# The second product of two MLPs with tokens on partitions, in 2x2 blocks with seven block products

## The chip, the cores and the metric

One core of a Trainium2 chip runs the whole program. The metric is the time of one execution in microseconds (us) on the device, as the median of several runs. The engines are TensorE (PE in the profile, its weight loads PEld), VectorE (DVE), ScalarE (ACT), GpSimd (POOL) and SyncE (SP, which here issues most of the loads). Each takes its own list of instructions; semaphores order them among each other.

## What is computed

512 tokens of 1024 features in float32 go through two layers, each a token mixer and a squared-ReLU MLP of width 4096, both with RMSNorm ahead and a residual behind. The first mixer is an attention with forget gates (FoX), the second a latent attention (MLA). Only the MLPs, their surroundings and the closing norm matter here:

```python
def sq_relu_mlp(h, w_up, w_down):
    return jnp.square(jax.nn.relu(h @ w_up)) @ w_down
for layer in range(DEPTH):
    ...
    x = x + sq_relu_mlp(rms_norm(x, norm_ffn_g[layer]), ffn_w_up[layer], ffn_w_down[layer])
    if layer == N_A_LAYERS - 1:
        k_nope, k_rope, v_shared = mla_shared_kv(x, kv_norm_g, mla_w_kv_a, mla_kv_a_norm_g, ...)
return rms_norm(x, final_norm_g)
```

## The kernel before

Activations lie with features on partitions: eight tiles of 128 features x 512 tokens. PE multiplies float32r, so every float32 operand is split into two float32r parts, hi (a cast on ACT) and lo (the difference, on DVE), and a product of two operands is three matmuls (`three`, L184): hi hi, hi lo, lo hi. With `flip` the operands change places, and the output has tokens on partitions.

The weights come in pieces of 128 x 1024 elements (512 KB) in the order of their use. `piece` (L174) hands out the next and starts the one behind it: a load on SP's queue into `raw` (two buffers), the cast to `whi` (L168) and the difference `wlo` (L169), with three buffers each. `linear` (L201) makes 24 matmuls of 512 tokens from a piece. Other operands are 2 KB tiles of a pool of 40 (`rt`, L104) or 14 (`rt2`); scratch tiles come from a pool of eight (`tt`, L107). PSUM's eight banks are shared under three tags for the whole program (L94).

The order within each engine's list is not that of the text: the framework places the instructions by the text's order, what is ready, and which buffers are free.

`ffn` (L580) goes through the width in four chunks of 1024. For each of a chunk's eight up pieces, `linear` fills a bank; DVE takes the larger of it and 0 times 1/rms of the token (L601), ACT squares twice (L603, L604), and DVE takes the difference (L605). Then come eight down pieces, each added to the residual by DVE (L617). The sum of squares for the next norm is built as each x is finished (`square_sum`, L212). `rstd_of` (L221) sums it over partitions with small matmuls (L226) and finds 1/rms by Newton steps on POOL or DVE; `along_tokens` (L246) spreads it over the partitions with matmuls (L251). The second MLP does its last chunk's down pieces twice, for 256 tokens each; `finish` (L629) closes the first half while the second is multiplied.

Between the MLPs, MLA makes its six inputs (L704 to L718), one after the other, from x scaled by two gains (`hk`, `hm`, L651); the norm of the keys' input needs the first two of them, and the first values (`v_gen`, L724) need that norm.

## Time and profile before

| | us |
|---|---|
| three runs, lowest to highest | 1173.04 to 1174.48 |
| their median | 1174.44 |
| span of the profiled execution, from its first to its last instruction | 1170.7 |
| first MLP, roughly | 262 to 612 |
| MLA's inputs and first values | 612 to 680 |
| second MLP, roughly | 809 to 1158 |

The profile gives the span of its execution and no other time for it; the median lies 3.7 us above that span. A row of the timeline starts with the start and the duration in us; in brackets stands how long the engine was idle before, and what released it. Matmuls overlap, so that the distance from start to start counts and not the duration of one. A row of a table by stretches has the stretch, its length, the busy us and instructions of PE, PEld, DVE, ACT and POOL, the granted clock of PE as a share, the DMA share and GB/s.

### The profile page before, as it was taken

To read this page: it belongs to the slowest core of one execution; us is meant where nothing else is said; L and a number is where in the kernel's file an instruction comes from. 1 tells how busy PE (TensorE), PEld (TensorE's weight loads), DVE (VectorE), ACT (ScalarE), POOL (GpSimd) and SP (SyncE) were. 2 spreads that over 40 slices of the span, in tenths; PEclk is the share of its full clock that TensorE was granted. 3 is DMA by queue.
4 is the path that set the end of the run, shared out by engine and by line. 5 is a ranking of instruction groups with operands and counts; after the bars stand their busy time and mean duration, and the time that the engine had idled before them with its cause. 6 is when DMAs were issued, how large, how long until landed. Compare 5 with 4: busy or idle time off the path is not lost.

```text
span 1170.7 us, 14430 instructions
## 1 busy us (share of the span) xinstructions
PE 1147.6 (98%) x5652; PEld 947.2 (81%) x5652; DVE 657.5 (56%) x1179; ACT 482.9 (41%) x839; POOL 28.9 (2%) x96
## 2 busy tenths in 40 slices
PE   8999999999999999999999999999999999999996
PEld 6777887788888888888887778788888888888895
DVE  6788887774434434334466688736433443433465
ACT  5555655553313223223344566534322322422441
POOL 1000000001000000000002100001000000000002
PEclk9999999999999999999999999999999999999998
DMA  5332222162232332323342211233322323223253
GB/s 183 128 108 73 73 90 76 34 198 90 91 107 90 93 106 90 104 94 93 124 144 80 59 39 50 73 108 114 102 90 93 105 90 104 95 91 107 90 175 113
DMA packets 35779, 116.13 MB, mean 99 GB/s; under 512 B 4080, under 2 KB 5744, under 8 KB 35712
## 3 DMA queue, kind: packets, MB, share of 16 engines
q1 hardware_dynamic: 34704, 113.62, 30.3%
q0 software_dynamic: 320, 1.05, 0.3%
q8 instruction: 44, 0.72, 0.3%
q10 hardware_dynamic: 688, 0.55, 0.1%
q14 instruction: 23, 0.19, 0.1%
HBM read 110.98 MB, written 4.23 MB: 98 GB/s over the span
## 4 chain that ended last, share of the span: by engine, by line
PE 94%; DVE 2%; POOL 1%; DMA 1%; ACT 1%; issue 1%; SPq 0%; DVEq 0%; ACTq 0%; POOLq 0%
PE acc L191 14%; PE acc L192 14%; PE acc L193 14%; PE sc L193 7%; PE sc L191 7%; PE sc L192 7%; PE tp L191 6%; PE tp L193 6%; PE tp L192 6%; PE tp L314 3%; PE sc L499 2%; PE sc L767 1%; PE acc L187 1%; PE acc L188 1%; PE acc L189 1%; PE tp L515 1%
## 5 line engine op out<-in xcount | busy, mean ns | idle before, releaser
L168 ACT CAST whi<-raw 128x1024 fp32r<-128x1024 f32 (+2 forms) x190 | 196.6, 1035 | 533.7 <-issue 234.6
L191 PE MATMUL acc<-r,whi 128*128 128x512 f32 (+1 forms) x780 | 303.2, 390 | 5.1 <-ACT whi L165 5.0
L193 PE MATMUL acc<-r,wlo 128*128 128x512 f32 (+1 forms) x780 | 298.1, 382 | 0.1
L192 PE MATMUL acc<-r,whi 128*128 128x512 f32 (+1 forms) x780 | 298.2, 383 | 0.0
L169 DVE TENSOR_TENSOR wlo<-raw,whi 128x1024 fp32r<-128x1024 f32 (+2 forms) x190 | 228.6, 1203 | 51.8 <-ACT whi L168 51.5
L191 PEld LDWEIGHTS acc<-r,whi 128*128 128x128 f32 x780 | 147.1, 189 | 35.4 <-ACT whi L165 5.0
L193 PEld LDWEIGHTS acc<-r,wlo 128*128 128x128 f32 x780 | 147.1, 189 | 29.2 <-DVE wlo L169 0.4
L192 PEld LDWEIGHTS acc<-r,whi 128*128 128x128 f32 x780 | 147.3, 189 | 28.0 <-DVE r L209 1.2
L191 PE MATMUL sc<-r,whi 128*128 128x512 f32 (+1 forms) x320 | 121.4, 379 | 0.0
L191 PE MATMUL tp<-r,whi 128*128 128x512 f32 (+1 forms) x320 | 121.3, 379 | 0.0
L193 PE MATMUL sc<-r,wlo 128*128 128x512 f32 (+1 forms) x320 | 121.1, 378 | 0.0
L193 PE MATMUL tp<-r,wlo 128*128 128x512 f32 (+1 forms) x320 | 121.1, 378 | 0.0
L192 PE MATMUL tp<-r,whi 128*128 128x512 f32 (+1 forms) x320 | 121.1, 378 | 0.0
L192 PE MATMUL sc<-r,whi 128*128 128x512 f32 (+1 forms) x320 | 121.1, 378 | 0.0
L192 PEld LDWEIGHTS tp<-r,whi 128*128 128x128 f32 x320 | 60.2, 188 | 11.3
L192 PEld LDWEIGHTS sc<-r,whi 128*128 128x128 f32 x320 | 60.2, 188 | 11.2
L191 PEld LDWEIGHTS tp<-r,whi 128*128 128x128 f32 x320 | 60.2, 188 | 11.2
L193 PEld LDWEIGHTS tp<-r,wlo 128*128 128x128 f32 x320 | 60.2, 188 | 11.2
L193 PEld LDWEIGHTS sc<-r,wlo 128*128 128x128 f32 x320 | 60.2, 188 | 11.2
L191 PEld LDWEIGHTS sc<-r,whi 128*128 128x128 f32 x320 | 60.2, 188 | 11.2
L301 ACT ACTIVATE t<-t,sm 128x512 f32<-128x512 f32 (+3 forms) x96 | 53.3, 558 | 32.6 <-DVE sm L297 32.2
L617 DVE TENSOR_TENSOR x<-x,acc 128x512 f32<-128x512 f32 (+1 forms) x32 | 19.9, 621 | 78.9 <-PE acc L193 78.9
(141 smaller groups left out, 1304.5 us busy)
## 6 DMA issues: line engine op xcount, KB each, us to landing
raw<-wts SPq DMA_DIRECT2D x186, 512.0 KB, 3.5
nb<-csc SPq DMA_DIRECT2D x8, 512.0 KB, 4.3
t<-xT SPq DMA_DIRECT2D x8, 256.0 KB, 6.1
x<-xT SPq DMA_DIRECT2D x8, 256.0 KB, 4.6
xkeep<-x SPq DMA_DIRECT2D x8, 256.0 KB, 2.0
x<-xkeep SPq DMA_DIRECT2D x8, 256.0 KB, 5.7
raw<-wts SPq DMA_DIRECT2D x4, 384.0 KB, 3.1
outT<-t POOLq DMA_DIRECT2D x4, 256.0 KB, 2.7
```

The lines of the kernel that those rows point to most:

```text
L168: nc.scalar.copy(hi[:, :w], raw[:, :w])
L169: nc.vector.tensor_tensor(lo[:, :w], raw[:, :w], f32(hi[:, :w]), op=ALU.subtract)
L187: mm(dst, xhi, whi, start=start, stop=False)
L188: mm(dst, xhi, wlo, start=False, stop=False)
L189: mm(dst, xlo, whi, start=False, stop=stop)
L191: mm(dst, whi, xhi, start=start, stop=False)
L192: mm(dst, whi, xlo, start=False, stop=False)
L193: mm(dst, wlo, xhi, start=False, stop=stop)
L301: nc.scalar.activation(out=Ls[e][:, :n], in_=Ls[e][:, :n], func=AF.Exp, scale=-1.0, bias=m[:, e : e + 1], accum_out=rs[:, e : e + 1])
L314: nc.tensor.transpose(tp[:, j * P : (j + 1) * P], L[:, j * P : (j + 1) * P], ident)
L499: mm(scs[e][:, :n], a[rows, q], b2[rows, :n], start=st, stop=sp)
L617: nc.vector.tensor_tensor(x[f][:, t], x[f][:, t], dn, op=ALU.add)
```

## The change

The first product of an MLP stays as it is. The second is computed as tokens x features: `three` with `flip`. Its inner dimension of 4096 is cut into eight parts of 512. For the first seven, the left operand (512 tokens x 512) and the right one (512 x 1024) are cut in 2x2 blocks, and seven block products are formed from the blocks and from sums and differences of them (`PRODUCTS`, in Winograd's form), in chunks of two, two, two and one parts; the up products of the next chunk are spread between the block products. The left blocks are squares from ACT (Relu, then Square); DVE makes the sums in place (`left`, `right`). Every operand is split behind that. Two of the products stay in four banks through all seven parts, two are gathered in SBUF (`q5`, `q7`), three are added to the output at each chunk's end. `combine` adds up the rest, and `plain` does the eighth part with the usual eight products of blocks.

1/rms now comes in as a factor per partition, squared, where a product is added to the output (`add_to`). The first MLP's output is turned back by 32 transposes (`turned_half`), with x kept in DRAM meanwhile (`xmid`); MLA's six inputs run in two passes over halves of the features, in the order `KORDER`. The second MLP's input is turned by 32 transposes, and the closing norm works on tokens by partitions, one block of 128 at a time. Residual tiles come from the pool of 40; PSUM is divided anew for each stage. The output has the shape (512, 1024), and the weights are laid out for it on the host. The diff, cut:

```diff
+HALF = 512
+CHUNKS = (2, 2, 2, 1)
+PRODUCTS = (("p1", "A11", "B11"), ("q5", "S1", "T1"), ("p6", "S2", "T2"), ("x3", "S4", "B22"), ("q7", "S3", "T3"), ("x2", "A12", "B21"), ("x4", "A22", "T4"))
+STRAIGHT = {"x2": (0, 0), "x3": (0, 1), "x4": (1, 0)}
+KORDER = (4, 5, 6, 7, 0, 1, 2, 3)
...
+    out += [("ffn0", 1024)] * 32
+    out += [("ka", 1024)] * 6
...
+    def stage(name, **tags):
+        if psum:
+            psum["stack"].close()
+        psum["stack"] = ExitStack()
+        psum["pool"] = psum["stack"].enter_context(
+            tc.tile_pool(name=f"ps_{name}", bufs=1, space=bass.MemoryType.PSUM, reuse_waits="tile")
+        )
+        psum["tags"] = tags
...
-    def rstd_of(acc, dim, mult=1.0, alone=False):
-        """acc: squares summed over blocks of features; -> mult/rms per token on a partition [128, 4]."""
+    def rstd_of(acc, dim, mult=1.0, tag="tp"):
         nb = acc.shape[-1] // P
-        ss = bank("tp", (P, nb))
+        ss = bank(tag, (P, nb))
         for tb in range(nb):
             mm(ss[:, tb : tb + 1], acc[:, tb * P : (tb + 1) * P], ones, start=True, stop=True)
+        return rsqrt_mean(ss, dim, mult)
+    def rsqrt_mean(ss, dim, mult=1.0, alone=False):
+        nb = ss.shape[-1]
...
-            xf = xpool.tile([P, S], F32, tag=f"x{f}", name=nm("x"))
+            xf = f32(rt())
...
+    def ffn(acc, layer, tokens, after):
+        gname = f"ffn{layer}"
+        base = DOWN + layer * DFF * D
+        with ExitStack() as fs:
+            rawp = fs.enter_context(tc.tile_pool(name="mlp_raw", bufs=8, reuse_waits="tile"))
+            sp = fs.enter_context(tc.tile_pool(name="mlp_s", bufs=4, reuse_waits="tile"))
+            h = [scaled(x[k], gname, k) for k in range(KD)]
+            state_ = {"r2": None}
+            s, raws, s1, zs = {}, {}, {}, {}
+            def up_item(n):
+                up = bank("go" if n < 4 * CHUNKS[0] and n % 2 else "up")
+                linear(up, piece(gname), h)
+                if state_["r2"] is None:
+                    rs = rstd_of(acc, D, tag="go")
+                    r2 = state_["r2"] = small.tile([P, NB], F32, tag="r2", name=nm("r2"))
+                    nc.vector.tensor_tensor(r2, rs, rs, op=ALU.mult)
+                hf, at = divmod(n, HALF // P)
+                if at == 0:
+                    s[hf] = sp.tile([P, HALF // P, S], F32, tag="s", name=nm("s"))
+                t = tt()
+                nc.scalar.activation(out=t, in_=up, func=AF.Relu)
+                nc.scalar.activation(out=s[hf][:, at, :], in_=t, func=AF.Square)
+            def raw(hf, a, b):
+                if (hf, a, b) not in raws:
+                    t = rawp.tile([P, 2, S], F32, tag="q", name=nm("q"))
+                    at = base + (hf * 4 + a * 2 + b) * P * 2 * S
+                    nc.sync.dma_start(t, wts[at : at + P * 2 * S].rearrange("(p j c) -> p j c", p=P, j=2))
+                    raws[hf, a, b] = t
+                return raws[hf, a, b]
+            def sub(out, a, b):
+                nc.vector.tensor_tensor(out, a, b, op=ALU.subtract)
+            def right(hf, kind):
+                b11, b12, b21, b22 = ((lambda a=a, b=b: raw(hf, a, b)) for a in range(2) for b in range(2))
+                if kind == "B11":
+                    return b11()
+                if kind == "T1":
+                    sub(b11(), b12(), b11())
+                    return b11()
+                if kind == "T2":
+                    sub(b11(), b22(), b11())
+                    return b11()
+                if kind == "B22":
+                    return b22()
+                if kind == "T3":
+                    sub(b12(), b22(), b12())
+                    return b12()
+                if kind == "B21":
+                    return b21()
+                if kind == "T4":
+                    sub(b11(), b21(), b11())
+                    return b11()
+            def left(hf, kind):
+                a11, a12, a21, a22 = (s[hf][:, k::2, t * 256 : (t + 1) * 256] for t in range(2) for k in range(2))
+                if kind == "S1":
+                    s1[hf] = sp.tile([P, 2, S // 2], F32, tag="s1", name=nm("s1"), bufs=2)
+                    nc.vector.tensor_tensor(s1[hf], a21, a22, op=ALU.add)
+                    return s1[hf]
+                if kind == "S2":
+                    sub(s1[hf], s1[hf], a11)
+                    return s1[hf]
+                if kind == "S4":
+                    sub(s1[hf], a12, s1[hf])
+                    return s1[hf]
+                if kind == "S3":
+                    sub(a21, a11, a21)
+                    return a21
+                return {"A11": a11, "A12": a12, "A22": a22}[kind]
+            held, filled = {}, set()
+            def add_to(tb, o, src):
+                dst, r = tokens[tb][o], state_["r2"][:, tb : tb + 1]
+                if layer == 0 and (tb, o) not in filled:
+                    nc.vector.tensor_scalar_mul(dst, src, r)
+                    filled.add((tb, o))
+                else:
+                    nc.vector.scalar_tensor_tensor(out=dst, in0=src, scalar=r, in1=dst, op0=ALU.mult, op1=ALU.add)
+            def down_item(chunk, i, hf):
+                to, lk, rk = PRODUCTS[i]
+                begin, end = hf == chunk[0], hf == chunk[-1]
+                kept = to[0] == "p"
+                if kept:
+                    begin, end = hf == 0, hf == starts[-1] - 1
+                    if begin:
+                        held[to] = [bank("keep"), bank("keep")]
+                elif begin:
+                    held[to, "bank"] = [bank("go"), bank("go")]
+                zs = held[to] if kept else held[to, "bank"]
+                rsrc = right(hf, rk)
+                whi, wlo = zip(*(split(rsrc[:, j, :]) for j in range(2)))
+                lsrc = left(hf, lk)
+                lhi, llo = (tt([P, 2, S // 2]).bitcast(F32R) for _ in range(2))
+                split(lsrc, lhi, llo)
+                for b in range(2):
+                    t = slice(b * P, (b + 1) * P)
+                    for j in range(2):
+                        three(zs[b], whi[j], wlo[j], lhi[:, j, t], llo[:, j, t], begin and j == 0, end and j == 1, flip=True)
+                if kept or not end:
+                    return
+                for b in range(2):
+                    if to in STRAIGHT:
+                        ta, o = STRAIGHT[to]
+                        add_to(2 * ta + b, o, zs[b])
+                    elif (to, b) not in held:
+                        held[to, b] = f32(rt())
+                        nc.scalar.copy(held[to, b], zs[b])
+                    else:
+                        nc.vector.tensor_tensor(held[to, b], held[to, b], zs[b], op=ALU.add)
+            def combine():
+                for b in range(2):
+                    u = tt()
+                    nc.scalar.copy(u, held["p1"][b])
+                    q5, q7 = held["q5", b], held["q7", b]
+                    u2 = tt()
+                    nc.vector.tensor_tensor(u2, u, held["p6"][b], op=ALU.add)
+                    add_to(b, 1, u2)
+                    add_to(b, 1, q5)
+                    nc.vector.tensor_tensor(u2, u2, q7, op=ALU.add)
+                    nc.vector.tensor_tensor(q5, q5, u2, op=ALU.add)
+                    add_to(2 + b, 1, q5)
+                    add_to(2 + b, 0, u2)
+                    add_to(b, 0, u)
+            def plain(hf):
+                ws, hs = {}, {}
+                for o in (1, 0):
+                    for k in range(2):
+                        t = raw(hf, k, o)
+                        ws[k, o] = [split(t[:, j, :]) for j in range(2)]
+                for ta in range(2):
+                    for k in range(2):
+                        lhi, llo = (rt((P, 2, S // 2)) for _ in range(2))
+                        hs[ta, k] = split(s[hf][:, k::2, ta * 256 : (ta + 1) * 256], lhi, llo)
+                order = [(tb, o) for o in (1, 0) for tb in range(NB)] if layer == 0 else [(tb, o) for tb in range(NB) for o in (1, 0)]
+                for tb, o in order:
+                    pp = bank("go")
+                    t = slice(tb % 2 * P, tb % 2 * P + P)
+                    for m in range(4):
+                        k, j = divmod(m, 2)
+                        lhi, llo = hs[tb // 2, k]
+                        three(pp, *ws[k, o][j], lhi[:, j, t], llo[:, j, t], m == 0, m == 3, flip=True)
+                    add_to(tb, o, pp)
+                    after(tb, o)
+            starts = np.concatenate([[0], np.cumsum(CHUNKS)]).tolist()
+            ends = starts[1:] + [starts[-1] + 1]
+            ups = [[hf * 4 + j for hf in range(a, b) for j in range(4)] for a, b in zip(starts, ends)]
+            for n in ups[0]:
+                up_item(n)
+            for c in range(len(CHUNKS)):
+                chunk = list(range(starts[c], starts[c + 1]))
+                items = [(i, hf) for i in range(7) for hf in chunk]
+                todo = list(ups[c + 1])
+                room = max(len(items) - 3, 1)
+                for m, (i, hf) in enumerate(items):
+                    while todo and (len(ups[c + 1]) - len(todo)) * room <= m * len(ups[c + 1]):
+                        up_item(todo.pop(0))
+                    down_item(chunk, i, hf)
+                assert not todo
+            combine()
+            plain(starts[-1])
+    stage("mlp0", up=1, go=3, keep=4)
+    xmid = keep.tile([P, KD, S], F32, name="xmid")
+    for k in range(KD):
+        nc.sync.dma_start(xmid[:, k, :], x[k])
+    xkeep = keep.tile([P, KD, S], F32, name="xkeep")
+    ytok = [[f32(rt()) for _ in range(2)] for _ in range(NB)]
+    xnew, hk, hm = {}, {}, {}
+    closing = {}
+    def turned_half(o):
+        if not closing:
+            closing["acc"] = tt()
+        for f in range(4 * o, 4 * o + 4):
+            xf = xnew[f] = f32(rt())
+            nc.sync.dma_start(xf, xmid[:, f, :])
+            pp = bank("go")
+            for tb in range(NB):
+                nc.tensor.transpose(pp[:, tb * P : (tb + 1) * P], ytok[tb][o][:, (f % 4) * P : (f % 4 + 1) * P], ident)
+            nc.vector.tensor_tensor(xf, xf, pp, op=ALU.add)
+            hk[f] = scaled(xf, "kv", f)
+            square_sum(closing["acc"], xf, f == KORDER[0])
+        for f in range(4 * o, 4 * o + 4):
+            hm[f] = scaled(xnew[f], "mix1", f)
+            nc.sync.dma_start(xkeep[:, f, :], xnew[f])
+    ffn(acc, 0, ytok, lambda tb, o: turned_half(o) if tb == NB - 1 else None)
+    acc = closing["acc"]
+    stage("mla", acc=3, sc=2, tp=3)
+    rpstack = ExitStack()
+    rp2 = rpstack.enter_context(tc.tile_pool(name="rp2", bufs=RP2, reuse_waits="tile"))
...
+        six = [bank(t) for t in ("acc", "sc", "sc", "acc", "tp", "tp")]
+        srcs = [hk, hk, hk, hm, hm, hm]
+        kv_t, q_t = [], []
+        for part in range(2):
+            for n in range(3):
+                w = blocks(piece("ka"))
+                for m in range(2):
+                    q = 2 * n + m
+                    for j in range(4):
+                        k = KORDER[4 * part + j]
+                        three(six[q], *w[4 * m + j], *srcs[q][k], part == 0 and j == 0, part == 1 and j == 3)
+                    if part == 0:
+                        continue
+                    if q == 0:
+                        rs = rstd_of(acc, D)
+                    elif q == 1:
+                        rstd = rstd_tile(rs)
+                        kv_t = [evac(t) for t in six[:2]]
+                        kv_acc = squares(kv_t)
+                    elif q == 2:
+                        krh, krl = roped(evac(six[2]))
+                    elif q == 3:
+                        rs = rstd_of(kv_acc, KVR)
+                        q_t.append(evac(six[3]))
+                    elif q == 4:
+                        ckv = normed(kv_t, rstd_tile(rs), "kva")
+                        q_t.append(evac(six[4]))
+                    else:
+                        q_t.append(evac(six[5]))
...
+    stage("mlp1", up=1, go=3, keep=4)
+    xtok = [[f32(rt()) for _ in range(2)] for _ in range(NB)]
+    fpool = ctx.enter_context(tc.tile_pool(name="fin", bufs=1, reuse_waits="tile"))
+    gfin = fpool.tile([P, D], F32, name="gfin")
+    nc.scalar.dma_start(gfin, fing.partition_broadcast(P))
+    sums = fpool.tile([P, 2, NB], F32, name="sums")
+    def finish(tb, o):
+        junk = tt()
+        nc.scalar.activation(out=junk, in_=xtok[tb][o], func=AF.Square, accum_out=sums[:, o, tb : tb + 1])
+        if o:
+            return
+        ss = small.tile([P, 1], F32, tag="ss", name=nm("ss"))
+        nc.vector.tensor_tensor(ss, sums[:, 0, tb : tb + 1], sums[:, 1, tb : tb + 1], op=ALU.add)
+        rs = rsqrt_mean(ss, D, alone=True)
+        for oh in (1, 0):
+            t = tt()
+            nc.vector.scalar_tensor_tensor(out=t, in0=xtok[tb][oh], scalar=rs, in1=gfin[:, oh * S : (oh + 1) * S], op0=ALU.mult, op1=ALU.mult)
+            q = (nc.sync, nc.scalar)[oh]
+            q.dma_start(out[tb * P : (tb + 1) * P, oh * S : (oh + 1) * S], t)
+    for tb in range(NB):
+        for o in range(2):
+            pp = bank("go")
+            for j in range(4):
+                nc.tensor.transpose(pp[:, j * P : (j + 1) * P], x[4 * o + j][:, tb * P : (tb + 1) * P], ident)
+            nc.scalar.copy(xtok[tb][o], pp)
+    ffn(acc, 1, xtok, finish)
+    psum["stack"].close()
+    assert state["next"] == len(PIECES)
```

More of the change, by code (lines that the diff above doesn't have):

```diff
@@ L113, in trunk @@
     mm = nc.tensor.matmul
+    stage("fox", acc=3, sc=2, tp=3)
     gsb = const.tile([P, NG], F32, name="gsb")
@@ L567, in out_proj @@
         return acc
-    rp2 = ctx.enter_context(tc.tile_pool(name="rp2", bufs=RP2))
+    x = []
+    acc = out_proj("fo", [parts[k] for k in range(KD)], xT, outs)
+    def ffn(acc, layer, tokens, after):
[155 more added lines that the diff above has]
+            plain(starts[-1])
@@ L645, in trunk @@
-    acc = ffn(acc, "ffn0", "ffn0")
-    xkeep = keep.tile([P, KD, S], F32, name="xkeep")
-    for k in range(KD):
-        nc.sync.dma_start(xkeep[:, k, :], x[k])
-    hk = [scaled(x[k], "kv", k) for k in range(KD)]
-    hm = [scaled(x[k], "mix1", k) for k in range(KD)]
-    xstack.close()
     ctxs = []
@@ L677, in roped @@
             return split(a)
-        banks = iter(["acc", "sc", "sc", "tp", "tp", "acc"])
-        def down(name, hs):
-            pp = bank(next(banks))
-            linear(pp, piece(name), hs)
-            return pp
         def evac(src):
```

144 lines of the change are left out of this document (27 added, 117 removed).

## The prediction

> **What bounds the kernel now.** I read the page first (busy shares, then the chain that ended last), then the busy time by stretches, then PE's waits.
>
> ```profile
> span 1170.7 us, 14430 instructions
> PE 1147.6 (98%) x5652; PEld 947.2 (81%) x5652; DVE 657.5 (56%) x1179; ACT 482.9 (41%) x839; POOL 28.9 (2%) x96
> ...
> PE 94%; DVE 2%; POOL 1%; DMA 1%; ACT 1%; issue 1%; SPq 0%; DVEq 0%; ACTq 0%; POOLq 0%
> ```
>
> ```profile
> 0.00:235.00 235.00, 227.82 (x1265) 181.84 (x1266) 185.54 (x466) 136.38 (x303) 4.77 (x20) 1.00 0.30 95
> 262.00:612.00 350.00, 350.00 (x1553) 290.05 (x1552) 151.99 (x179) 110.77 (x145) 3.28 (x12) 1.00 0.33 102
> ```
>
> After the span the second table's columns are PE, PEld, DVE, ACT, POOL and the granted clock: in the first MLP (262 to 612) PE never rests, while DVE works 152 of 350 us. In the FoX stage DVE is at 185.54/235 = 79% and PE still loses only 7 us, most of it at the start. So each product that goes is worth its full pace, as long as DVE and ACT feed PE. What that pace is:
>
> ```profile
> 563.28 0.39 PE L191 MATMUL tp<-r,whi 128*128 128x512 f32 x1
> ...
> 568.72 0.39 PE L191 MATMUL acc<-r,whi 128*128 128x512 f32 x1
> ```
>
> ```profile
> 651.30 0.39 PE L187 MATMUL acc<-whi,r 128*128 128x512 f32 x1
> ...
> 651.98 0.39 PE L187 MATMUL acc<-whi,r 128*128 128x512 f32 x1
> ```
>
> ```profile
> 1110.09 0.28 PE L191 MATMUL acc<-r,whi 128*128 128x256 f32 x1
> ...
> 1112.48 0.28 PE L193 MATMUL acc<-r,wlo 128*128 128x256 f32 x1
> ```
>
> From the first to the second row lie 24 products: 5.44/24 = 0.2267 us each (the 0.39 overlap). With the operands exchanged (L187, the form that the change uses) three take 0.68, the same. With 256 columns twenty take 2.39, 0.1195 each, where half of 0.2267 is 0.1134.
>
> **The change, part by part.** *Products.* Each MLP has 32 pieces up and 32 down, 24 products each: 1536. Afterwards: 768 up; down, seven of eight 512-row parts with seven block products of 12 each (84 instead of 96), one part plain: 588 + 96 = 684. That is 84 fewer for each MLP, 168 x 0.2267 = **-38.1 us**. The last chunk in halves goes: 384 products x (0.1195 - 0.1134) = **-2.3**.
>
> ```profile
> 274.20 0.89 PE tp L251 x8
> ...
> 762.92 0.87 PE tp L314 x8
> ...
> 1145.83 0.71 PE tp L251 x4
> ...
> 1159.47 0.62 PE tp L226 x4
> ```
>
> These rows of the chain price the turning. The output now has tokens on partitions, so 32 transposes come at the end of the first MLP and 32 at the start of the second: 64 x 0.87/8 = **+7.0**. The row 1/rms along tokens is no longer built in the MLPs (two times 0.89), nor the first half's closing norm (about 0.62 + 0.71): **-3.1**.
>
> *The end.*
>
> ```profile
> 1157.77 0.28 PE L193 MATMUL acc<-r,wlo 128*128 128x256 f32 x1
> ...
> 1160.19 0.16 DVE L228 TENSOR_SCALAR rs<-tp 128x2 f32<-128x2 f32 x1 [0.77 <-PE tp L226]
> ...
> 1162.43 0.16 DVE L237 SCALAR_TENSOR_TENSOR rs<-rs,rs 128x2 f32<-128x2 f32 x1
> ...
> 1163.90 3.22 DVE L638 SCALAR_TENSOR_TENSOR t<-x,gsb,tp 128x256 f32<-128x256 f32 x8 [1.32 <-PE tp L251]
> ```
>
> From the last product's end (1158.05) to 1170.7 are 12.65 us. Afterwards: handover 0.3, add 0.7, square with its sum 0.9, sum of two 0.2, the same twelve small operations 2.4, two scalings of 512 columns 1.4, and the store as now (1167.12 to 1170.7, 3.6): 9.5, so **-3.1**.
>
> *VectorE, the price of the scheme.*
>
> ```profile
> 628.32 0.69 DVE L688 TENSOR_TENSOR t<-acc,rstd 128x512 f32<-128x512 f32 x1 [1.93 <-ACT rstd L257]
> 628.93 0.68 DVE L688 TENSOR_TENSOR t<-sc,rstd 128x512 f32<-128x512 f32 x1
> ```
>
> ```profile
> 563.48 0.69 DVE L601 SCALAR_TENSOR_TENSOR t<-tp,rstd 128x512 f32<-128x512 f32 x1 [2.71 <-PE tp L193]
> 564.38 1.22 DVE L169 TENSOR_TENSOR wlo<-raw,whi 128x1024 fp32r<-128x1024 f32 x1 [0.21 <-ACT whi L168]
> 565.53 0.68 DVE L605 TENSOR_TENSOR r<-t,r 128x512 fp32r<-128x512 f32 x1
> ```
>
> Start to start, DVE takes 0.61 for 512 columns and 1.15 for 1024. A block product needs three splits of 512 (1.8), T1 to T4 add 1.15, S1 to S4 0.6: 1.8 to 3.6 us, against 12 x 0.2267 = 2.72 of PE. The 5.44 us of each up product lie between them, with 1.15 of DVE. By chunks (PE / DVE): the first two 81.6 / 54, the third, with four up products instead of eight, 59.9 / 50, the last 40.8 / 30. The first two are below the FoX stage's 79%, so I cost them at nothing; the third is at 83%, for which I take 1.5 us in each MLP (from 0 to 5): **+3**.
>
> The weak place is behind the last chunk. After its last up product four block products are left, 10.9 us of PE. In that time DVE has in its order: the rest of x4's splits 1.8, eight evacuations 4.9, the sixteen operations of `combine` 9.8, then the eight weight splits of `plain` 4.9 and a first left split 0.6: 22. Perhaps 3 of that is done while `combine` waits for q7. PE then stands 22 - 10.9 - 3 = 8 us in each MLP: **+16** (bounds 0, if the splits of `plain` go first, and 22).
>
> A PE that stands loses clock too:
>
> ```profile
> 1160.00:1162.00 2.00, 0.08 (x1) 0.00 (x0) 1.46 (x9) 0.00 (x0) 0.00 (x0) 0.78 0.00 0
> 1162.00:1164.00 2.00, 1.22 (x4) 0.93 (x4) 0.58 (x4) 0.00 (x0) 0.00 (x0) 0.50 0.00 0
> ```
>
> The granted clock was 1.00 until PE ran dry at 1158, 0.78 on average two to four us later, then 0.50. How long it stays low under new work no row shows. I take as long as it took to fall, 3 us at half pace, 1.5 lost, for the two holes and the one below: **+4.5** (bounds 0 and 22, all of one `plain` at half pace). The Trainium skill, "TensorE: Matmul & The Clock Gate", Part 1, says that an idle window of about 3.4 us halves the clock, and that as long a busy one restores it; the fall agrees with the two rows. By its figure each hole would lose an estimated 1.7 us instead of 1.5, and the sum would be 0.6 us higher.
>
> *Start of MLA.* Its six inputs now run in two passes over halves of k (72 products each), so the first MLP's last features can arrive late; but 1/rms and the keys' norm come later.
>
> ```profile
> 617.68 0.95 PE L226 MATMUL tp<-ones,t 128*128 128x1 f32 x8
> ...
> 626.50 1.16 PE L251 MATMUL tp<-ident,rs 128*128 128x128 f32 x8 [2.27 <-POOL rs L243]
> ```
>
> ```profile
> 638.40 0.95 PE L226 MATMUL tp<-ones,t 128*128 128x1 f32 x8
> ...
> 644.84 1.16 PE L251 MATMUL tp<-ident,rs 128*128 128x128 f32 x8
> ```
>
> ```profile
> PE sc L191 <- ACT r L139: 1.0, 1, 1.0
> ```
>
> ```profile
> 660.92 1.16 PE L251 MATMUL tp<-ident,rs 128*128 128x128 f32 x8 [1.38 <-POOL rs L243]
> ```
>
> The norm chain (L226 to L251) takes 8.8 or 6.4 us. Now the first values (L187, 651.30) start 39.1 us after the MLP's last product (612.24). Afterwards: transposes 1.7, first pass 16.3, one output 2.7, chain about 7.5, to the keys' squares 4.5, second chain with its sum 7.4, norm and split about 4.3: 44.4, so +5.3. The queries' later waits (1.4 and 1.0) then have time: -2.4. Without the transposes already counted: **+1.2**. The operand pool holds 40 tiles; at each MLP's start the eight token tiles come before h in it: +1 each, **+2** (bounds 0 and 5).
>
> *Sum:* -38.1 - 2.3 + 7.0 - 3.1 - 3.1 + 3 + 16 + 4.5 + 1.2 + 2 = **-12.9**. The span of 1170.7 becomes 1157.8. The runs' median of 1174.44 lies 3.7 above the span; I keep that: **1161.5 us**.
> ```profile
> x<-xT SPq DMA_DIRECT2D x8, 256.0 KB, 4.6
> xkeep<-x SPq DMA_DIRECT2D x8, 256.0 KB, 2.0
> ```
>
> Transfers cost nothing: the weights are fetched once, at the 102 GB/s of the row above, on SP's queue as now. The eight stores and eight loads of `xmid` that come on it are of the size of these two; the stores lie beside the first up products, and the last four loads, which wait for operand tiles, land some 5 us after the plain part, beside the first pass of 16.3 us. Without that cover they would cost those 5.
>
> **Rivals.** *A, everything is covered.* The orders of DVE and ACT are made so that the splits of `plain` go ahead of `combine`: neither hole, clock nor third chunk, only -38.1 - 2.3 + 7.0 - 3.1 - 3.1 + 1.2 = -38.4: 1136. For it: 79% of DVE in FoX and a full PE. Against it: 22 us of work against 10.9.
>
> *B, slower: ACT's order.* Every up product is followed by a Relu and a Square on ACT, and the splits of the next block product are written behind them. If they also run behind them, PE stands after each up product that a block product follows, 24 times in each MLP.
>
> ```profile
> 563.30 1.05 ACT L168 CAST whi<-raw 128x1024 fp32r<-128x1024 f32 x1 [3.34 <-issue]
> 564.26 0.63 ACT L603 ACTIVATE r<-t 128x512 fp32r<-128x512 f32 x1
> 564.78 0.61 ACT L604 ACTIVATE t<-t 128x512 f32<-128x512 f32 x1
> ```
>
> ACT's 512 columns start every 0.52 us; Relu, Square and three casts are 2.6, times 48: +125 in place of the holes, 1174.4 - 36.4 + 125 = 1263. It decides from 36.4/48 = 0.76 us a place. Against it: the cast at 563.30 starts as a piece ends (563.28) and the third of its buffers comes free, so it is that of three pieces on; the text has it behind that ended piece's squares, yet it runs before them. The order is not the text's, and casts run ahead as far as buffers reach: 12 operand tiles beside those held, three block products. For it: that lead is short, and a queue that is once placed wrongly stays so (2.27 us at 626.50 is such a place). The Trainium skill's same page says in Part 2 that ScalarE and VectorE take their queues strictly in order. No run here shows the opposite, and the price above is for just that.
>
> *C, DVE lags through chunks three and four,* about 0.5 us more for each of their 42 block products: +21, 1182. It needs DVE at 100% where I count 83%.
>
> **How the numbers follow.** Forecast 0.47 (1147 to 1172), A 0.25 (1135 to 1147), B and C with its neighbourhood 0.20 (above 1177), between them 0.08, of which 0.06 lie within the 0.2%. Range 1136 to 1184: from A, which leaves nothing to cover, to C; only B's full form lies outside. A measurement tells 0.2%, 2.3 us, from no change: faster 0.74, same 0.06, slower 0.20.
>
> **What would show it.** Products in the profile: 168 fewer of 512 columns' worth, at 0.227 a piece; a wait of PE for DVE ahead of the plain part, 8 us, in both MLPs, with the clock at 0.5 behind it; about 9.5 us from the last product to the end; first values of MLA some 5 us later than now after the MLP's last product. Wrong it is if PE waits after up products (B), if DVE is at 95% in the third chunk (C), or if PE goes from Strassen's last product straight on to the plain part (A).

## The result and the profile after

The changed kernel takes 1270.62 us (median of four, 1269.95 to 1272.38), the kernel before 1173.74 beside it (1171.68 to 1174.48): the ratio is 1.0836, with a 95% interval of 1.0821 to 1.0852. It is slower by 97 us, where 12.9 less were forecast. The profiled execution has a span of 1269.1 us.

From the page of the changed kernel: its span, the engines' busy shares, and the engines in the chain that ended last.

```profile
span 1269.1 us, 14402 instructions
PE 1142.4 (90%) x5324; PEld 913.7 (72%) x5324; DVE 828.7 (65%) x1482; ACT 596.4 (47%) x1103; POOL 18.9 (1%) x80
...
PE 64%; DVE 6%; ACT 6%; issue 1%; DMA 1%; POOL 1%; DVEq 0%; SPq 0%; POOLq 0%; ACTq 0%
```

PE has less to do than before and stands longer: 127 us without work, 23 before. In the chain its share fell from 94% to 64%, but the shares of that row add up to 79% only, so that the row can't say what took the rest. No engine is full: DVE is at 65%, ACT at 47%. So no other engine became the bound; there are many waits. PE's waits in the changed kernel (us in total, times, longest):

```profile
PE up L203 <- ACT t L616: 61.0, 46, 1.4
PE go L201 <- DVE r L153: 12.2, 2, 8.2
PE sc L203 <- DVE r L790: 9.6, 1, 9.6
PE go L200 <- DVE r L153: 8.0, 1, 8.0
...
PE go L199 <- DVE r L790: 3.4, 1, 3.4
PE go L199 <- ACT t L152: 3.4, 2, 1.9
```

The first row has the sign of rival B: 46 times a product into `up` waits for the Relu (L616) of the up piece before. In the timeline of PE the place looks like this:

```profile
320.24 0.39 PE L203 MATMUL up<-r,whi 128*128 128x512 f32 x1
...
324.78 0.39 PE L205 MATMUL up<-r,wlo 128*128 128x512 f32 x1
326.57 0.50 PE L203 MATMUL up<-r,whi 128*128 128x512 f32 x1 [1.41 <-ACT t L616]
326.91 0.39 PE L204 MATMUL up<-r,whi 128*128 128x512 f32 x1
327.14 0.40 PE L205 MATMUL up<-r,wlo 128*128 128x512 f32 x1
327.37 0.39 PE L199 MATMUL go<-r,t 128*128 128x512 f32 x1
```

At 320.24 two block products have ended, and the rest of an up piece runs, until its last product at 324.78. What comes next on PE is not the block product that the text has there, but the first three products (L203 to L205) of the *next up piece*, and only then the block product (L199, into `go`). Those three need the bank `up`, the only one of its kind, and Relu hasn't read it out yet. The place costs 1.79 - 0.23 = 1.56 us start to start, and 0.11 at the next product. The mean of the 46 waits is a little shorter (61.0/46 = 1.33 against 1.41), so about 1.6 us a place, some 73 us in all.

The timeline of all engines over the same time says why Relu is late:

```profile
324.98 1.04 ACT L180 CAST whi<-raw 128x1024 fp32r<-128x1024 f32 x1 [9.51 <-PE up L204]
325.93 0.59 ACT L616 ACTIVATE t<-up 128x512 f32<-128x512 f32 x1
326.05 1.23 DVE L181 TENSOR_TENSOR wlo<-raw,whi 128x1024 fp32r<-128x1024 f32 x1 [9.86 <-ACT whi L180]
326.42 0.61 ACT L152 CAST t<-s 128x512 fp32r<-128x512 f32 x1
```

ACT and DVE have both been idle for over 9 us, and then everything comes at once. ACT's first instruction is the cast of a later weight piece (L180). Its buffer comes free with the ended piece's last L204, one product before the piece itself ends; so it stands ahead of Relu, for 0.95 us. Behind Relu stands the left split (L152) of the block product that should have run meanwhile. Its operand, a sum of two blocks (L656), was made by DVE at 287.43, long before.

### The profile page after: what moved, and what is told of

The parts are those of the page before. It is cut to its first block, busy times and chain, and to the rows that moved or that the text cites. A ratio compares the mean times of both kernels' runs of the same rounds, so it can differ in the third digit from the quotient of the medians.

```text
span 1269.1 us, 14402 instructions
## 1 busy us (share of the span) xinstructions
PE 1142.4 (90%) x5324; PEld 913.7 (72%) x5324; DVE 828.7 (65%) x1482; ACT 596.4 (47%) x1103; POOL 18.9 (1%) x80
## 4 chain that ended last, share of the span: by engine, by line
PE 64%; DVE 6%; ACT 6%; issue 1%; DMA 1%; POOL 1%; DVEq 0%; SPq 0%; POOLq 0%; ACTq 0%
PE up L203 9%; PE up L204 8%; PE up L205 7%; PE go L201 5%; PE go L199 5%; PE go L200 5%; ACT whi L180 3%; PE acc L203 2%; PE keep L199 2%; PE acc L204 2%; DVE r L678 2%; PE keep L200 2%; ACT t L616 2%; PE keep L201 2%; PE acc L205 2%
## 5 line engine op out<-in xcount | busy, mean ns | idle before, releaser
L180 ACT CAST whi<-raw 128x1024 fp32r<-128x1024 f32 (+2 forms) x118 | 120.4, 1022 | 301.9 <-PE up L204 203.5
L203 PE MATMUL up<-r,whi 128*128 128x512 f32 x448 | 180.1, 402 | 61.6 <-ACT t L616 61.0
L152 ACT CAST r<-q 128x512 fp32r<-128x512 f32 x212 | 126.8, 622 | 115.7 <-PE go L200 57.0
L204 PE MATMUL up<-r,whi 128*128 128x512 f32 x448 | 175.8, 392 | 3.6 <-DVE r L221 3.6
L205 PE MATMUL up<-r,wlo 128*128 128x512 f32 x448 | 175.1, 391 | 0.0
L153 DVE TENSOR_TENSOR r<-q,r 128x512 fp32r<-128x512 f32 x212 | 141.1, 687 | 35.9 <-ACT r L152 13.7
L203 PEld LDWEIGHTS up<-r,whi 128*128 128x128 f32 x448 | 84.4, 188 | 96.8 <-ACT t L616 80.5
L203 PE MATMUL acc<-r,whi 128*128 128x512 f32 x300 | 123.0, 413 | 5.0 <-ACT whi L177 5.0
L204 PE MATMUL acc<-r,whi 128*128 128x512 f32 x300 | 118.4, 396 | 0.0
L205 PE MATMUL acc<-r,wlo 128*128 128x512 f32 x300 | 118.4, 395 | 0.0
L199 PE MATMUL go<-r,t 128*128 128x512 f32 x280 | 110.0, 394 | 3.4 <-ACT t L152 3.4
L200 PE MATMUL go<-r,t 128*128 128x512 f32 x280 | 110.3, 394 | 0.0
L201 PE MATMUL go<-r,t 128*128 128x512 f32 x280 | 109.6, 393 | 0.0
L204 PEld LDWEIGHTS up<-r,whi 128*128 128x128 f32 x448 | 84.6, 189 | 20.5 <-DVE r L221 4.9
L205 PEld LDWEIGHTS up<-r,wlo 128*128 128x128 f32 x448 | 84.6, 189 | 17.7
L203 PEld LDWEIGHTS acc<-r,whi 128*128 128x128 f32 x300 | 57.1, 191 | 18.3 <-ACT whi L177 5.0
L205 PEld LDWEIGHTS acc<-r,wlo 128*128 128x128 f32 x300 | 56.9, 190 | 12.5 <-issue 0.4
L204 PEld LDWEIGHTS acc<-r,whi 128*128 128x128 f32 x300 | 57.1, 190 | 11.5 <-DVE r L221 1.2
```

What stands on the lines that cost most here:

```text
L152: nc.scalar.copy(hi, src)
L153: nc.vector.tensor_tensor(lo, src, f32(hi), op=ALU.subtract)
L180: nc.scalar.copy(hi[:, :w], raw[:, :w])
L199: mm(dst, xhi, whi, start=start, stop=False)
L200: mm(dst, xhi, wlo, start=False, stop=False)
L201: mm(dst, xlo, whi, start=False, stop=stop)
```

## The experiments

The runs, told in the order of the argument, fall into three groups: what makes the 46 waits, what makes the holes between the stages, and what the form is worth alone. "Before" was between 1171.7 and 1173.4 us beside them.

### E1: Relu without a scratch tile

On the changed kernel. Relu's tile `t` is one of the scratch pool of eight, from which the left splits take theirs too.

```diff
-                t = tt()
-                nc.scalar.activation(out=t, in_=up, func=AF.Relu)
-                nc.scalar.activation(out=s[hf][:, at, :], in_=t, func=AF.Square)
+                nc.scalar.activation(out=s[hf][:, at, :], in_=up, func=AF.Relu)
+                nc.scalar.activation(out=s[hf][:, at, :], in_=s[hf][:, at, :], func=AF.Square)
```

> The changed kernel (1270.6) with one edit: Relu writes into the square's own tile and Square works there, so that an up product takes no scratch tile. Theory P (the places of the scratch pool are given out in the text's order, so the left split of the next block product stands behind the Relu of the up product before it; PE therefore turns to the next up product and meets the one bank that this Relu must free): the 46 waits of PE for ACT's Relu in the bank 'up' (61 us, 1.33 each) fall to under 10, block products stand whole between up products, and about 46 x 1.6 = 73 us go: 1190 to 1210. Rival Q (ACT's queue: the cast of a later weight piece runs ahead of the Relu, whatever is between): the cast still runs first and at least half of the waits stay, 1235 or more. The hole ahead of the plain part stays under both (about 20 us over the two MLPs).

1189.25 us (ratio to before 1.0146, 1.0129 to 1.0163): 81.4 less for the same work. All 46 waits are gone. ACT's timeline, and PE's, of this run:

```profile
302.95 1.14 ACT L152 CAST t<-s 128x512 fp32r<-128x512 f32 x2
...
317.02 0.62 ACT L152 CAST t<-s 128x512 fp32r<-128x512 f32 x1 [2.10 <-PE keep L200]
322.46 1.05 ACT L180 CAST whi<-raw 128x1024 fp32r<-128x1024 f32 x1 [4.82 <-PE up L204]
323.42 0.59 ACT L615 ACTIVATE s<-up 128x512 f32<-128x512 f32 x1
```

```profile
317.05 0.39 PE L203 MATMUL up<-r,whi 128*128 128x512 f32 x1
...
322.49 0.39 PE L199 MATMUL go<-r,t 128*128 128x512 f32 x1
...
325.21 0.39 PE L203 MATMUL up<-r,whi 128*128 128x512 f32 x1
```

Now the left splits run up to three block products ahead. Up to 317.02 six of them have started in this MLP, one before the rows shown, and the block product at 322.49 is the third: its split is one of the pair at 302.95, 19 us earlier. The one at 317.02 is for a product further on, and waits only for a place that an ended block product frees (L200, into `keep`). The block product starts right behind the piece (322.49), and the next piece only at 325.21. The cast (322.46) still stands ahead of Relu, and it costs nothing: Relu is done at 324.01, 1.2 us before `up` is needed. So the cast's place alone is not the cause.

The same run answers rival C. A stretch in the second chunk of the first MLP, and the third chunk (stretch, length, PE, PEld, DVE, ACT, POOL, granted clock, DMA share, GB/s):

```profile
400.00:470.00 70.00, 70.00 (x311) 57.98 (x310) 48.27 (x67) 36.50 (x60) 0.00 (x0) 1.00 0.35 113
470.00:532.00 62.00, 62.00 (x275) 51.38 (x274) 51.55 (x73) 31.88 (x52) 0.00 (x0) 1.00 0.33 102
```

DVE is at 51.55/62 = 83% in the third chunk, as counted, and PE never rests. Nor does it in the fourth up to 560, with DVE at 17.53/28 = 63%.

### E9: The left splits in another pool

The other party moves: Relu keeps its scratch tile, and the left splits take theirs from the pool of 40.

```diff
-                lhi, llo = (tt([P, 2, S // 2]).bitcast(F32R) for _ in range(2))
+                lhi, llo = (rt((P, 2, S // 2)) for _ in range(2))
```

> The changed kernel with another cure of the same cause: Relu keeps its scratch tile, and the left splits of the block products take their two tiles from the pool of 40 instead. Under P (one pool's places given out in the text's order to Relu and to the left split behind it) the 46 waits for the Relu go as in E1, though the pool of 40 now serves six tiles a block product, so that the lead is two products and not three: 1188 to 1205. If E1's gain came from Relu and Square working in place (fewer tiles, another timing on ACT) and not from the order of the places, the waits stay: 1260 or more.

1194.32 us (1.018, 1.0162 to 1.0199), and again no wait for Relu. Each of the two edits alone takes the waits away, so it is the pool that they share: a left split gets its place there only behind the Relu ahead of it in the text, and that Relu waits for PE. It is the order and not a lack of places: in the changed kernel the first two block products have ended at 320.24, so that no left split holds a place any more, and ACT is idle until 324.98; yet the split of the block product at 327.37 comes only at 326.42, behind the Relu. How the framework counts the places is not in a trace; that sharing them does it is shown from both sides.

### E3: Two banks for the up products

```diff
-                up = bank("go" if n < 4 * CHUNKS[0] and n % 2 else "up")
+                up = bank("go" if n % 2 else "up")
```

> The changed kernel with up products alternating between the bank 'up' and one of the three 'go' banks throughout, not only in the first eight. Theory R (the one bank is what PE waits for): the waits for the Relu go, some 60 us less, about 1205, and no new wait as large comes, since block products need two 'go' banks at a time. Theory P allows it too, but then PE, past the first products of the next up piece, meets the left split, which is still behind Relu and cast: some 0 to 1 us of the 1.33 come back each time, 1205 to 1250. If block products now lack the third 'go' bank: waits in 'go' for VectorE, above 1250.

1215.87 us (1.0371, 1.0351 to 1.0392), 54.8 less. Of the 46 waits eight are left:

```profile
PE up L203 <- ACT t L616: 11.2, 8, 1.4
```

The three products that run ahead find a free bank. The order stays wrong, and mostly costs nothing.

### E2: The cast one product later

The last reader of `whi` in `three` becomes the piece's last product, so that the cast into that buffer can't stand ahead of Relu.

```diff
-            mm(dst, whi, xlo, start=False, stop=False)
-            mm(dst, wlo, xhi, start=False, stop=stop)
+            mm(dst, wlo, xhi, start=False, stop=False)
+            mm(dst, whi, xlo, start=False, stop=stop)
```

> The changed kernel with the second and third of an up product's three matmuls exchanged, so that the weights' hi tile is read by the very last one and its place comes free no earlier than the bank. Under P and Q alike the Relu then runs ahead of the cast: each of the 46 waits shrinks from 1.33 to about 0.4 (the cast takes 0.96), about 44 us less, 1225 to 1232, with the number of waits unchanged (P). If the cast is not what delays the Relu, nothing changes: 1270.

1239.85 us (1.0576, 1.0555 to 1.0597), 30.8 less; 1225 to 1232 was expected. The waits of this run:

```profile
PE up L203 <- ACT t L616: 32.0, 46, 0.7
```

The 46 waits stay and halve, from 1.33 to 0.70 on average. The miss is Relu itself, which takes 0.59 and can't be hidden when the next product needs its bank at once. These runs give the three links: the shared pool decides the order (81), the single bank makes it a wait (55), the cast doubles that wait (31). They overlap, and don't add up.

### E4: The weight splits of `plain` first

The other waits. On the changed kernel, the eight weight splits of `plain` are written ahead of `combine`.

```diff
+            ws = plain_weights(starts[-1])
             combine()
-            plain(starts[-1])
+            plain(starts[-1], ws)
```

> The changed kernel with the eight weight splits of the plain part written ahead of the sixteen operations of combine. If the hole ahead of the plain part (12.0 us and 8.2 us of waits for VectorE's split) is VectorE's order, as forecast, it shrinks to under 3 us in each MLP, and with the lost clock behind it some 18 to 25 us go: 1246 to 1252. If the splits wait for places of the operand pool or for the weights' load, the hole stays: 1265 to 1272. The 46 waits for the Relu stay in both.

1261.63 us (1.0762, 1.0733 to 1.0791): 9.0 less, and 1246 to 1252 was expected. PE's waits there:

```profile
PE go L201 <- DVE r L153: 14.4, 2, 9.4
```

The hole fell from 20.2 us (12.2 + 8.0) to 14.4 only. In this run's DVE timeline one sees what the edit passed over:

```profile
592.06 6.13 DVE L153 TENSOR_TENSOR r<-q,r 128x512 fp32r<-128x512 f32 x9 [0.88 <-PE keep L200]
...
618.84 2.49 DVE L153 TENSOR_TENSOR r<-s,r 128x512 fp32r<-128x512 f32 x4
```

The weight splits (of `q`) now run early. The four left splits (of `s`) are still written behind `combine`, run behind it, and PE needs the first of those as well.

### E5: All splits of `plain` first

On E1: the eight weight splits and the four left splits ahead of `combine`.

```diff
+            parts_ = plain_weights(starts[-1])
             combine()
-            plain(starts[-1])
+            plain(starts[-1], *parts_)
```

> E1's kernel (1189.2) with the eight weight splits and the four left splits of the plain part ahead of combine. In E4 the hole only moved behind the left splits, which stood behind combine still. Theory H (VectorE's order sets the hole): the waits of PE for VectorE's split ahead of the plain parts (16.7 us in E1) fall under 3 us; with the lost clock behind them 14 to 20 us go, if the additions of combine do not now keep the three 'go' banks of the plain part busy: 1169 to 1176. If the splits wait for places of the operand pool: over 10 us of waits stay, 1183 to 1190.

1170.24 us (0.9981, 0.9971 to 0.9991): 19.0 less than E1, and both holes are gone from PE's waits.

### E6: The turning back in its own banks

On E1: `turned_half` shares `go` with `plain`; here it takes the free banks of `keep`.

```diff
-            pp = bank("go")
+            pp = bank("keep")
```

> E1's kernel with the transposes of the first MLP's output in the four 'keep' banks, free by then, instead of the three 'go' banks that the plain part's second half and MLA's inputs need. Theory B (banks): the waits ahead of the plain part's second half (3.4 us) and of MLA's inputs (9.1 us) go, with the clock lost behind them 13 to 18 us: 1171 to 1177. Rival S (each residual tile's load waits for a place of the pool of 40, which comes free only after the store of the one before; eight loads in a row of some 4.4 us each): PE then waits later, at the inputs' second pass, and only 3 to 7 us go: 1182 to 1186.

1178.65 us (1.0059, 1.004 to 1.0077): 10.6 less, between what the two theories gave. Both hold: the waits in the middle of `plain` are gone, and another stays ahead of MLA:

```profile
PE tp L203 <- DVE r L789: 6.7, 1, 6.7
```

What that is shows SP's queue in E1:

```profile
597.40 0.33 SPq L794 DMA_DIRECT2D xkeep<-r  x1
597.77 0.43 SPq L785 DMA_DIRECT2D r<-xmid  x1
601.48 0.32 SPq L794 DMA_DIRECT2D xkeep<-r  x1
601.84 0.43 SPq L785 DMA_DIRECT2D r<-xmid  x1
```

Each load of x from DRAM (L785) goes out right behind the store of the x before it (L794); the seven of them in this queue are four to seven us apart. That fits a pool of 40 with one place left, which the store frees; E8 puts it to the test.

### E7 and E8: Both, and the loads of x in other tiles

E5 and E6 in one kernel:

> E5 and E6 together. If the two holes are separate, the gains add: under H and B 1152 to 1163; under H with S 1162 to 1170; the block products would then be ahead of the kernel before (1171.7 to 1173.7).

1159.78 us (0.9905, 0.9884 to 0.9925). On top of that, the loads of x take the tiles of the raw weights, which are free by then:

```diff
-            xf = xnew[f] = f32(rt())
+            xf = xnew[f] = psum["q"].tile([P, 2, S], F32, tag="q", name=nm("q"))[:, 0, :]
```

> E7 with the residual tiles that are turned back in the MLP's raw weight tiles (eight, free by then) instead of the pool of 40, so that the eight loads of xmid need not follow each other. Under S what is left of MLA's wait goes: 5 to 12 us below E7. Under B alone nothing changes against E7 (within 2 us).

1154.15 us (0.9841, 0.9817 to 0.9865), 5.6 less, and the wait of 6.7 is gone, as it should be if the pool's last place held the loads apart.

### E10: The layout without the seven products

On E8: all eight parts as eight plain block products. What is left out is the form alone, its sums and its 84 fewer products in each MLP.

```diff
-            for c in range(len(CHUNKS)):
...
-            combine()
-            plain(starts[-1], *parts_)
+            for hf in range(DFF // HALF):
+                part(hf, list(range(4 * hf + 4, min(4 * hf + 8, DFF // P))))
```

> E8 with all eight parts of the second product done with eight products of blocks (the weights and the left operand split once each), so that the tokens on partitions, the turning, the two passes and the closing stay, and the seven-product form goes: no sums of blocks, no gathering, no combine. 168 products more at 0.2267 are +38.1, less E8's last waits at the plain part (about 2 us): 1186 to 1193 if the form brings in E8 what its products weigh, and then the layout by itself costs 13 to 20 us against the kernel before. If the form's extra work on VectorE and ScalarE takes part of that back in E8, this kernel lies closer to E8: under 1180.

1200.47 us (1.0233, 1.0219 to 1.0247), 46.3 above E8; 1186 to 1193 was expected. 38.1 are the 168 products. Of the other 8, most is a wait of this kernel's own, for a split:

```profile
PE go L199 <- ACT r L152: 6.2, 1, 6.2
```

So by this one pair the form is worth about its 38 us where PE is fed, and the layout that it needs costs up to 27 by itself (1200.5 - 1173.4), 6 of them in this wait. The edit of E11 is not in this kernel, so that the 27 are an upper figure.

### E11: The second MLP's input turned later

On E8: the 32 transposes (L996 in the changed kernel) behind the third up piece, instead of ahead of the first.

```diff
+                if n == 2 and between:
+                    between()
...
-    ffn(acc, 1, xtok, finish)
+    ffn(acc, 1, xtok, finish, turn_in)
```

> E8 with the 32 transposes and eight copies of the second MLP's input written behind its third up product instead of ahead of the first. In E8 PE waits 2.8 us for the split of h at that place and runs the next some 4 us at a lower clock. If the copies on ACT ahead of h's casts cause it, 3 to 6 us go: 1148 to 1151. If it is the places of the pool (x, h and the token tiles together), it stays: 1153 to 1156.

1145.63 us (1141.86 to 1150.19; 0.9768, 0.9741 to 0.9794): 8.5 less than E8, a little over the 3 to 6 expected; the runs of each of the two kernels spread over 7 to 8 us, so that the 8.5 is good to a few us. PE's wait of 2.8 for the split of h is gone. Its page, with a span of 1143.8 us:

```profile
PE 1117.5 (98%) x5324; PEld 912.2 (80%) x5324; DVE 817.5 (71%) x1482; ACT 601.0 (53%) x1103; POOL 19.4 (2%) x80
```

The same 5324 products as in the changed kernel, PE back at 98%, and 2.3% under the kernel before. The steps from 1270.6 to it: the shared scratch pool 81.4, DVE's order at `plain` 19.0, the banks of the turning 10.5 (E6 alone: 10.6), the place in the pool of 40 5.6, the turning ahead of the second MLP 8.5; 125.0 together.

## Why the prediction was wrong

**The step that failed** is the one against rival B: "The order is not the text's, and casts run ahead as far as buffers reach: 12 operand tiles beside those held, three block products." That holds for weight splits, which live in the pool of 40, and it is where I looked. A block product also needs a left split. Its place lies in the scratch pool of eight, behind the Relu tile of the piece ahead, and so it can't run ahead by even one (E1 and E9). "The 5.44 us of each up product lie between them" held for PE, where 24 products lie between two block products. But the left split could use none of that time, and three of the 24 were already the next piece's, which met a single `up` bank.

Rival B had this place right: a split of the next block product does run behind the Relu, and its sign, that PE waits after up products, came true. That its number, 1263, came out near 1270.6 is luck. It has 48 places at 2.6 us, with Relu, Square and three casts in a row, and no holes. Measured are 46 places at 1.6 us, with the weight cast and Relu in a row, and the holes on top. Its turning point, 0.76 us a place, was passed. The Trainium skill ("TensorE: Matmul & The Clock Gate", Part 1, on the depths of the engines' queues) calls the queues of ACT and DVE strictly first in, first out. The rows of ACT agree as far as they go: cast, Relu and left split run one behind the other (324.98, 325.93, 326.42), though the split's operand had been there since 288.

**Products: held.** 5324 matmuls stand in the profile instead of 5652; of the difference, 168 are the form's, since E10, which does without it, has 5492. The flipped ones go at 0.2267 us: a block product of 12 takes 322.49 to 325.21, 2.72 us, in E1.

**Third chunk, +3: not needed** (E1). C fell.

**Hole ahead of `plain`, 8 each: mechanism right, size off in the first MLP.** Two gaps there, and one in the second MLP:

```profile
621.84 0.80 PE L200 MATMUL go<-r,r 128*128 128x512 f32 x1 [8.02 <-DVE r L153]
626.66 0.79 PE L201 MATMUL go<-r,r 128*128 128x512 f32 x1 [4.02 <-DVE r L153]
627.25 0.63 PE L199 MATMUL go<-r,r 128*128 128x512 f32 x1
...
629.68 0.40 PE L199 MATMUL go<-r,r 128*128 128x512 f32 x1
...
1235.81 0.80 PE L201 MATMUL go<-r,r 128*128 128x512 f32 x1 [8.17 <-DVE r L153]
```

12.0 us and 8.2. The difference of 22 - 10.9 without the 3 that I deducted is 11.1; the deduction fits the second MLP only.

**Clock: right in kind, more often.** Behind the hole, seven products take from 626.66 to 629.68, 3.02 us instead of 1.59: 1.4 lost, where 1.5 was taken. In the second MLP eleven take 4.78 us from 1235.81 on, instead of 2.49: 2.3 lost. And there were more gaps than the three counted. Reckoned the same way from the rows of PE, 2.5 are lost behind the wait at 644.78, 3.1 from 714.65 on, 1.5 from 879.10 on, and 1.6 in the place that the last section shows: 12.4 in six places, where 4.5 was taken.

**The turning, +7 and "the last four loads ... land some 5 us after the plain part, beside the first pass": mis-sized.** The loads were called covered. In fact they come one by one (E6, with SP's queue), and the transposes hold the banks of `plain` on top. From the last product of the first MLP's `plain` to the first values of MLA, 44.4 us were forecast. In the changed kernel, and behind it in E8:

```profile
657.99 0.40 PE L201 MATMUL go<-r,r 128*128 128x512 f32 x1
...
714.65 0.65 PE L199 MATMUL acc<-whi,r 128*128 128x512 f32 x1 [2.11 <-ACT r L152]
```

```profile
595.74 0.40 PE L201 MATMUL go<-r,r 128*128 128x512 f32 x1
...
639.36 0.80 PE L199 MATMUL acc<-whi,r 128*128 128x512 f32 x1 [2.11 <-ACT r L152]
```

56.3 us, counted from the end at 658.39, and 43.2 once banks and pool are right. The estimate of the stage was good; the buffers were left out of it.

**The end: held.** From 1258.69, the last product's end, to 1269.1 are 10.4 us; forecast 9.5.

```profile
1258.30 0.39 PE L201 MATMUL go<-r,r 128*128 128x512 f32 x1
```

Of the 109 us between the forecast (1161.5) and the result, the 46 waits are some 73, the stage behind the first MLP 12, the larger hole 4, the wait in `plain` for the turning's banks 3.4, two waits for left splits behind the last up pieces 3.4, and the clock behind the gaps some 8 more than was counted. About 5 us have no row of their own, or 8, since the 3 for the third chunk were not needed; some 2 of them are waits for the splits of h at the start of an MLP (4.1 where 2 was taken), and what the others are stays open. E1's 81.4 are those 73, the two waits for left splits (3.4), and 3.5 of the hole ahead of `plain` (16.7 us there, 20.2 in the changed kernel), so that they don't explain the rest. Rival A's 1136 was not reached either: the best kernel is 9.6 us above. In its trace PE works at half clock from 640.4 and from 667.7, 6.8 us each, and has work throughout, so that an estimated 6.8 of them are clock; what the gaps ahead of these two places are worth was not tried.

## What to carry to other kernels

Ask of every buffer that an operation running ahead needs, and not only of the largest pool, who stands before it in the order in which the places are given out. If that one waits for the engine that is to be kept busy, the operation can't run ahead, however idle its own engine is: here ACT and DVE had stood for 9 us. Moving work that feeds the bound engine ahead of work that doesn't only pays if all of its operands are moved (E4 against E5), and an algorithm with fewer products is judged only when that is done: the same 5324 products took 1270.6 us and 1145.6.

## What was unexpected of the hardware

A short gap can cost clock after it has ended. In the changed kernel PE stood for 1.91 us and then started at full pace. The timeline of PE, and windows of 1 us with the granted clock as the third number from the end:

```profile
600.80 0.50 PE L199 MATMUL go<-r,t 128*128 128x512 f32 x1 [1.91 <-ACT t L152]
...
602.07 0.51 PE L199 MATMUL go<-r,t 128*128 128x512 f32 x1
...
605.71 0.39 PE L201 MATMUL go<-r,t 128*128 128x512 f32 x1
```

```profile
602.00:603.00 1.00, 1.00 (x4) 0.75 (x4) 1.00 (x2) 0.83 (x2) 0.00 (x0) 0.60 0.81 283
603.00:604.00 1.00, 1.00 (x4) 0.79 (x3) 0.65 (x2) 0.00 (x0) 0.00 (x0) 0.50 0.61 242
...
605.00:606.00 1.00, 1.00 (x5) 0.82 (x4) 0.83 (x2) 0.33 (x1) 0.00 (x0) 0.69 0.03 8
```

A mean of 0.60 is 0.8 us at half clock, one of 0.69 is 0.6 us: so it fell at 602.2, 1.4 us after work had begun again, while PE was busy without a break, and came back at 605.6, 3.4 us later. From 602.07 to 605.71 nine products took 3.64 us instead of 2.04: the gap of 1.91 us cost 1.6 more. The 1.41 us at the up piece left the pace at full: behind it the rows from 326.91 on follow at 0.23.

The length of the gap alone doesn't decide. E3 has the same gap, of 1.91 us too, and there the clock stayed at 1.00:

```profile
572.75 0.50 PE L199 MATMUL go<-r,t 128*128 128x512 f32 x1 [1.91 <-ACT t L152]
```

```profile
573.00:574.00 1.00, 1.00 (x5) 0.80 (x5) 0.78 (x2) 1.00 (x3) 0.00 (x0) 1.00 0.11 20
...
576.00:577.00 1.00, 1.00 (x6) 0.83 (x5) 1.00 (x2) 0.21 (x1) 0.00 (x0) 1.00 0.03 8
```

The Trainium skill ("TensorE: Matmul & The Clock Gate", Part 1) has a window of about 3.4 us that runs freely, whenever the work starts. Both traces agree with it: in each of them, all changes of the clock lie whole multiples of 3.41 us apart (602.2, 605.6, 615.85 and 629.5 in the changed kernel; E3's next is at 588.67). Counted back on these grids, the gap of the changed kernel (598.89 to 600.80) lies whole in the window from 598.79 to 602.20, at whose end the clock falls, and that of E3 (570.84 to 572.75) on both sides of a boundary at 571.60. A shorter gap of the changed kernel, 1.49 us (1213.40 to 1214.89), lies whole in a window too and left the clock at 1.00. So it mattered how much of one window was idle; where exactly the limit lies, these few gaps don't tell.
